# Modulation blocks 40 to 87 summed with multiply-adds on DVE during layer 0's feed-forward part, instead of matmuls on TensorE

## The chip, the cores and the metric

The kernel runs on one core of one Trainium2 chip. The metric is the device time of one execution in microseconds (us); lower is better. The engines are called PE (TensorE, with PEld for its weight loads), DVE (VectorE), ACT (ScalarE), POOL (GpSimd) and SP (SyncE, which here issues nearly all large loads).

## What is computed

Two layers of a transformer over 256 latent and 256 context tokens, width 1024, all in fp32. This case is about the modulation: for each layer, six vectors of 1024 numbers for each of two kinds of tokens.

```
silu_l = jax.nn.silu(c)
silu_c = jax.nn.silu(c_ctx)[None, :]
for layer in range(DEPTH):
    mod_l = split(silu_l @ mod_w[layer] + mod_b[layer], 6)
    mod_c = split(silu_c @ mod_w[layer] + mod_b[layer], 6)
    hl = modulate(rms_norm(xl, norm1_g[layer]), mod_l[0], mod_l[1])
    ...
    xl = xl + mod_l[2] * mix_l
    xl = xl + mod_l[5] * channel_mix(modulate(rms_norm(xl, norm2_g[layer]), mod_l[3], mod_l[4]))
    if need_ctx:          # layer 0 only; the same for xc with mod_c[2..5]
```

`channel_mix` is a SwiGLU of width 2816 in layer 0 (below: the feed-forward part) and a mixture of eight experts, two for each token, in layer 1. After layer 1's mixer the context tokens are no longer used.

## The kernel before

**Modulation.** Layers (`l`), vectors (`g`, 0 to 5) and slices of 128 inputs (`k`, 0 to 7) make 96 blocks of 128x1024 weights, 512 KB each, numbered j = 48 l + 8 g + k. `mod_load` issues a block's load on SP into a ring of buffers, named `rm` in the trace; `mod_ring` sets which buffers the ring has and up to which block it may load. A ring's buffer is loaded anew only when the block in it has been used. `tick()` uses one block: four matmuls on PE (line 458), in which `sc`, the two silu vectors padded to 32 columns, is the stationary operand and 256 columns of the block each are moved past it, added up over the eight k in one PSUM bank. After k = 7 `tick_end` copies the bank to SBUF on ACT (line 466), transposes it on PE (line 469) and adds the bias on DVE (line 473) into `modc`; `gain` (line 423) forms 1 + scale times the norm's gain.

**Where ticks stand.** Blocks 0 to 39 are used during layer 0's mixer. `norm_last`, the normalisation that ends a mixer or the feed-forward part, takes a pair of tick counts, one for each half of the tokens: (1, 3) ahead of the feed-forward part, and the rest up to block 71 after it. In the feed-forward part there is one tick after each of its blocks. Blocks 72 to 87 are used in layer 1's mixer, with a ring of one buffer, and 88 to 95 (layer 1, g = 5) behind it. A scheduler orders the code between `manual_schedule` sections and may bring ready instructions forward; each engine then runs its instructions in that order.

**The feed-forward part.** Weight blocks of 1 MB (`raw`) are loaded by SP into two buffers and split into a high part on ACT (`whi`, line 260) and a low part on DVE (`wlo`, line 273). Each product is three fp32r matmuls of 512 columns (`mm3`, lines 577 to 579). `FFN_PARTS` cuts the width 2816 in three parts; each has 4, 4 or 3 up-blocks b (256 columns of w1 and of w3: 96 matmuls each) and then four down-blocks. The first up-block is special: its input comes out of the normalisation just before, one k of eight at a time. For each k, `norm_pair` does two multiplications on DVE (`xn`, line 564), the high part on ACT (`hhi`, line 565), the low part on DVE (`hlo`, line 566), and then PE does the twelve matmuls of that k.

**Layer 1.** After the mixer the experts' weights, most of the kernel's bytes, are streamed in by SP. The first buffers for them come free when layer 1's scores (line 1407) have read `xT` for the last time, and when the mixer's pools close.

Of the kernel before, what the change touches and what calls it, by code (L numbers as in the profile page):

```python
# [10 lines left out]
F32 = mybir.dt.float32  # L11
# [4 lines left out]
OP = mybir.AluOpType  # L16
# [122 lines left out]
def program(tc, a, out):  # L139
    nc = tc.nc  # L140
    V, A, P, TE = nc.vector, nc.scalar, nc.gpsimd, nc.tensor
    uid = [0]

    def nm(s):
        uid[0] += 1
        return f"{s}_{uid[0]}"
# [12 lines left out]
    def bank(tag="m"):  # L159
        return ps.tile([128, 512], F32, name=nm("pm"), tag=tag, bufs=3 if tag == "m" else 1)  # L160
# [237 lines left out]
    def col(n, j, w=1):  # L398
        o = _OFF[n] + j
        return par[:, o:o + w]  # L400
# [17 lines left out]

    def gain(l, n):
        g = col('norm1_g' if n == 0 else 'norm2_g', 8 * l, 8)  # L420
        for s in range(2):
            c = 8 + 24 * n
            V.scalar_tensor_tensor(gm[:, l, n, s, :], modc[:, l, s, c:c + 8], 1.0, g, op0=OP.add, op1=OP.mult)

# [4 lines left out]
    def mod_ring(ring, upto):  # L429
        rings[:] = ring  # L430
        mst[3] = upto
        mod_load(mst[0] + len(ring) - 1)

    def mod_load(j):
        while mst[0] <= min(j, mst[3] - 1):
# [9 lines left out]
            mraw[mst[0]] = r  # L445
            mst[0] += 1

    def tick(n=1, end=True):

        for _ in range(n):  # L450
            j = mst[1]
            mst[1] += 1
            l, g, k = mods[j]
            if k == 0:
                mst[2] = bank("t")
            r = mraw.pop(j)
            for i in range(4):
                TE.matmul(mst[2][32 * i:32 * i + 32, :256], sc[:, k, :], r[:, i * 256:(i + 1) * 256],  # L458
                          start=k == 0, stop=k == 7)
            mod_load(j + len(rings))  # L460
            if k == 7 and end:
                tick_end()
# [588 lines left out]
    mx.close()  # L1051
    fx = ExitStack()
    ap = fx.enter_context(tc.tile_pool(name="ap", bufs=8, reuse_waits="tile"))
    mod_ring([(mq, "rm", 2)] * 2 + [(ap, "rm", 6)] * 6, 72)

    def resid1(l, n, d, p, s):
        u = HALVES[s]
# [35 lines left out]
    for m0, mn in FFN_PARTS:  # L1093
        act = []
        for b in range(mn // 2):
            if m0 + b == 0:
                p1, p3 = [bank(), bank()], bank2()
                h.append(norm_pair(pb, 0, 1, 0))
                for k in range(KD):
                    if k + 1 < KD:  # L1100
                        h.append(norm_pair(pb, 0, 1, k + 1))
                    for (bh, bl), pq in zip(first, (p1, (p3[:, 0, :], p3[:, 1, :]))):
                        for m in range(2):
                            c = slice(m * 128, m * 128 + 128)
                            mm3(pq[m], bh[:, k, c], bl[:, k, c], h[k][0], h[k][1], k == 0, k == KD - 1)
                ws.split_to(ws.pos[2])
                order.close()
            else:
                bh, bl = take()
                p1 = [bank(), bank()]  # L1110
                for m in range(2):
                    c = slice(m * 128, m * 128 + 128)
                    for k in range(KD):
                        mm3(p1[m], bh[:, k, c], bl[:, k, c], h[k][0], h[k][1], k == 0, k == KD - 1)
                bh, bl = take()
                p3 = bank2()
            for m in range(2):
                c = slice(m * 128, m * 128 + 128)
                s = ap.tile([128, T], F32, name=nm("fs"), tag="fs", bufs=2)
                A.activation(s, p1[m], AF.Silu)  # L1120
                if m0 + b:
                    for k in range(KD):
                        mm3(p3[:, m, :], bh[:, k, c], bl[:, k, c], h[k][0], h[k][1], k == 0, k == KD - 1)
                V.tensor_tensor(s, s, p3[:, m, :], op=OP.mult)
                n = len(act) % 4
                if n == 0:
                    ah, al = wide("ah"), wide("al")
                hi, lo = ah[:, n, :], al[:, n, :]
                hilo(hi, lo, s)
                act.append((hi, lo))  # L1130
            tick()
        for b in range(4):
            bh, bl = take()
            for m in range(2):
                c = slice(m * 128, m * 128 + 128)
                d = 2 * b + m
                p = bank()
                for k in range(mn):
                    mm3(p, bh[:, k, c], bl[:, k, c], act[k][0], act[k][1], k == 0, k == mn - 1)
                if m0 < 16:  # L1140
                    resid(0, 1, d, p)
                elif d < KD - 1:
                    if d == 0:
                        pn = norm_begin()
                    resid(0, 1, d, p)
                    norm_sq(pn, d)
            if m0 < 16 or b < 3:
                tick()
            if m0 == 16 and b == 0:
                warm_sqrt()  # L1150
    order = ExitStack()
    order.enter_context(tc.manual_schedule(engines=ENGINES))
    pb = norm_last(0, 1, p, pn, (1, 71 - mst[1]))
    fx.close()
    hx.close()

# [752 lines left out]
```

## Time and profile before

| | |
|---|---|
| median of 3 runs | 1715.19 us (1713.47 to 1717.45) |
| profiled execution, its own time | 1716.25 us |
| its span in the profile | 1714.2 us |
| PE busy | 1618.4 us, 94% of the span |
| DVE busy | 767.3 us, 45% |
| ACT busy | 580.5 us, 34% |
| chain that ended last | PE 67%, DMA 20%, DVE 8% |

A chain that ended last is followed back from the last instruction, at each step to what released it. A matmul in fp32 stands in the trace as two instructions, one in fp32r as one. Times in the rows below are counted from the span's start.

### The profile page before, as it was taken

How to read it: one execution, taken by the hardware profiler on the slowest of the kernel's cores; microseconds unless marked ns; L12 is line 12 of the kernel's file. 1: busy time of each engine (PE TensorE's matmuls, PEld its weight loads, DVE VectorE, ACT ScalarE, POOL GpSimd, SP SyncE). 2: the span in 40 equal slices, each digit the busy share in tenths (PEclk: the TensorE clock that was granted, in tenths of full speed). 3: DMA queues.
4: the chain of work that ended last, by engine and by line, in shares of the span. 5: the costliest groups of instructions: out<-in, count | busy, mean ns of one | idle time of the engine just before them, and what ended most of it. 6: DMA issues, size and time to landing. Idle time of an engine off the chain costs nothing.

```text
span 1714.2 us, 21413 instructions
## 1 busy us (share of the span) xinstructions
PE 1618.4 (94%) x8369; PEld 1029.0 (60%) x8369; DVE 767.3 (45%) x1214; ACT 580.5 (34%) x872; POOL 112.7 (7%) x81
## 2 busy tenths in 40 slices
PE   6898889999999999989999998999999899999986
PEld 2675667887777776776843434776343357843322
DVE  6679856333333235767730002885201068830001
ACT  3465743322222123554420103675000156630000
POOL 1433210000000000341000000000000000000000
PEclk9998999999999999999999999999999999999999
DMA  9535324223233333553599999998999999989997
GB/s 356 202 121 172 124 99 178 105 98 123 98 101 133 111 105 127 174 209 132 220 394 415 421 424 424 424 424 333 424 424 424 424 424 424 397 342 423 425 423 303
DMA packets 79278, 476.03 MB, mean 278 GB/s; under 512 B 8561, under 2 KB 12017, under 8 KB 31105
## 3 DMA queue, kind: packets, MB, share of 16 engines
q1 hardware_dynamic: 76544, 468.25, 68.8%
q0 software_dynamic: 1536, 5.28, 0.8%
q8 instruction: 68, 1.11, 0.3%
q10 hardware_dynamic: 1088, 1.05, 0.2%
q14 instruction: 42, 0.34, 0.1%
HBM read 471.40 MB, written 3.15 MB: 277 GB/s over the span
## 4 chain that ended last, share of the span: by engine, by line
PE 67%; DMA 20%; DVE 8%; issue 2%; ACT 2%; SPq 0%; POOL 0%; DVEq 0%; ACTq 0%
DMA raw<-in_moe_w_dram 18%; PE pm L1736 9%; PE pm L577 7%; PE pm L578 7%; PE pm L579 6%; PE p L578 5%; PE p L577 5%; PE p L579 5%; PE p L1736 4%; PE pm L1756 3%; PE pm L1758 3%; PE pm L1755 3%; PE pm L458 2%; PE pm L950 1%; PE pm L940 1%
## 5 line engine op out<-in xcount | busy, mean ns | idle before, releaser
L260 ACT ACTIVATE whi<-raw 128x1024 fp32r<-128x1024 f32 (+2 forms) x285 | 289.3, 1045 | 293.8 <-PE pm L578 115.3
L273 DVE TENSOR_TENSOR wlo<-raw,whi 128x1024 fp32r<-128x1024 f32 (+2 forms) x254 | 298.4, 1209 | 200.8 <-ACT whi L260 192.9
L1736 PE MATMUL pm<-raw,xs 128*64 128x512 f32 (+1 forms) x1432 | 308.6, 555 | 15.2 <-DMA raw<-in_moe_w_dram 14.7
L1736 PEld LDWEIGHTS pm<-raw,xs 128*64 128x64 f32 x1432 | 107.9, 138 | 196.7 <-issue 155.2
L1855 DVE TENSOR_TENSOR es<-es,pm 128x512 f32<-128x512 f32 (+1 forms) x38 | 24.5, 644 | 334.2 <-PE pm L1736 302.2
L1736 PE MATMUL p<-raw,ats 128*64 128x512 f32 x648 | 159.1, 598 | 4.3 <-DMA raw<-in_moe_w_dram 3.7
L273 POOL TENSOR_TENSOR wlo<-raw,whi 128x1024 fp32r<-128x1024 f32 (+1 forms) x31 | 75.4, 2444 | 560.0 <-ACT k L1236 486.0
L1767 ACT ACTIVATE ats<-pm 128x512 f32<-128x512 f32 (+1 forms) x24 | 13.1, 544 | 278.5 <-PE p L1736 242.0
L577 PE MATMUL pm<-hhi,whi 128*128 128x512 f32 x240 | 96.4, 407 | 3.8 <-ACT hhi L565 3.8
L1736 PEld LDWEIGHTS p<-raw,ats 128*64 128x64 f32 x648 | 46.1, 136 | 88.7 <-issue 72.0
L578 PE MATMUL pm<-hlo,whi 128*128 128x512 f32 x240 | 97.2, 405 | 1.0 <-DVE hlo L566 1.0
L579 PE MATMUL pm<-hhi,wlo 128*128 128x512 f32 x240 | 96.2, 402 | 0.0
L1756 PE MATMUL pm<-wlo,xe 128*128 128x512 f32 x224 | 92.4, 412 | 4.0 <-DVE wlo L273 4.0
L1755 PE MATMUL pm<-whi,xe 128*128 128x512 f32 x224 | 88.0, 399 | 3.1 <-ACT whi L260 3.1
L577 PE MATMUL p<-hhi,whi 128*128 128x512 f32 x224 | 89.0, 398 | 1.3 <-ACT hhi L556 0.7
L578 PE MATMUL p<-hlo,whi 128*128 128x512 f32 x224 | 89.1, 398 | 0.0
L579 PE MATMUL p<-hhi,wlo 128*128 128x512 f32 x224 | 88.8, 396 | 0.0
L1848 ACT ACTIVATE es<-pm 128x512 f32<-128x512 f32 (+1 forms) x38 | 21.3, 559 | 151.6 <-PE pm L1736 146.1
L458 PE MATMUL pm<-rm,sc 128*32 128x256 f32 x768 | 61.5, 408 | 10.2 <-DMA rm<-in_mod_w_dram 9.0
L577 PE MATMUL pm<-ah,whi 128*128 128x512 f32 x176 | 70.2, 402 | 0.0
L578 PE MATMUL pm<-al,whi 128*128 128x512 f32 x176 | 69.6, 397 | 0.0
L579 PE MATMUL pm<-ah,wlo 128*128 128x512 f32 x176 | 69.0, 396 | 0.0
(450 smaller groups left out, 2589.1 us busy)
## 6 DMA issues: line engine op xcount, KB each, us to landing
raw<-in_moe_w_dram SPq DMA_DIRECT2D x322, 1024.0 KB, 19.0
rm<-in_mod_w_dram SPq DMA_DIRECT2D x96, 512.0 KB, 4.6
raw<-in_ffn_w_dram SPq DMA_DIRECT2D x30, 1024.0 KB, 4.8
raw<-in_ab_w_in_dram SPq DMA_DIRECT2D x7, 1024.0 KB, 6.8
raw<-in_cd_w_in_dram SPq DMA_DIRECT2D x6, 1024.0 KB, 6.7
whi<-in_moe_w_dram SPq DMA_DIRECT2D x12, 512.0 KB, 15.3
raw<-in_ab_w_out_dram SPq DMA_DIRECT2D x4, 1024.0 KB, 5.2
raw<-in_cd_w_out_dram SPq DMA_DIRECT2D x4, 1024.0 KB, 4.9
```

The source lines that it names most:

```text
L260: x = A.activation(h, c, AF.Copy)
L273: x = low.tensor_tensor(l, r, h.bitcast(F32), op=OP.subtract)
L458: TE.matmul(mst[2][32 * i:32 * i + 32, :256], sc[:, k, :], r[:, i * 256:(i + 1) * 256], start=k == 0, stop=k == 7)
L577: TE.matmul(p, wh, xh, start=first, stop=False)
L578: TE.matmul(p, wh, xl, start=False, stop=False)
L579: TE.matmul(p, wl, xh, start=False, stop=last)
L1736: TE.matmul(o if len(w.shape) == 2 else o.rearrange("p (a b) -> p a b", b=S), x, w, start=start, stop=stop)
L1755: TE.matmul(p, xh[:, k, :], bh[:, k, :], start=hf == 0 and k == 0, stop=False)
L1756: TE.matmul(p, xh[:, k, :], bl[:, k, :], start=False, stop=False)
L1758: TE.matmul(p, xl[:, k, :], bh[:, k, :], start=False, stop=hf == 1 and k == 3)
L1848: A.activation(s[:, :w], p1[:, :w], AF.Silu)
L1855: V.tensor_tensor(s[:, :w], s[:, :w], p3[:, :w], op=OP.mult)
```

## The change

Blocks 40 to 87 go through a new function, `tick_dve`. For each block and each kind of token it multiplies the 128x1024 block by the kind's silu value of each partition and adds it to an accumulator `ma` of the same shape, on DVE. After k = 7, eight matmuls with a column of ones (each takes 128 columns of `ma` as stationary operand and moves one column) sum over the partitions and leave the vector in a PSUM bank, in the layout that `modc` has; no transpose follows. For layer 1 and g of 2 and above only the latent kind is computed. So 48 blocks become 9 first multiplications (`TENSOR_SCALAR`) and 63 multiply-adds (`SCALAR_TENSOR_TENSOR`) of 128x1024, and 9 sets of 8 ones-matmuls. All 48 blocks are placed in the feed-forward part (two ticks after an up-block, three after a down-block, four in the `norm_last` before it), with a ring of five buffers instead of eight. None are left in the `norm_last` after it and none of 72 to 87 in layer 1's mixer, since `tick` now returns when the ring's last block is used up.

```diff
     def gain(l, n):
         g = col('norm1_g' if n == 0 else 'norm2_g', 8 * l, 8)
-        for s in range(2):
+        for s in range(2 if l == 0 or n == 0 else 1):
...
+    ON_DVE, macc = range(40, 88), []
+
+    def tick_dve(j, l, g, k):
+
+        kinds = range(2 if l == 0 or g < 2 else 1)
+        if k == 0:
+            macc[:] = [ap.tile([128, 1024], F32, name=nm("ma"), tag=f"ma{s}", bufs=2 - s) for s in kinds]
+        r = mraw.pop(j)
+        for s in kinds:
+            if k == 0:
+                V.tensor_scalar(macc[s], r, sc[:, k, s:s + 1], None, op0=OP.mult)
+            else:
+                V.scalar_tensor_tensor(macc[s], r, sc[:, k, s:s + 1], macc[s], op0=OP.mult, op1=OP.add)
+        mod_load(j + len(rings))
+        if k < 7:
+            return
+        q = bank("t")
+        for s in kinds:
+            for i in range(8):
+                TE.matmul(q[:, 8 * s + i:8 * s + i + 1], macc[s][:, i * 128:(i + 1) * 128], ones[:, 0:1], start=True, stop=True)
+            V.tensor_tensor(modc[:, l, s, 8 * g:8 * g + 8], q[:, 8 * s:8 * s + 8], col('mod_b', 48 * l + 8 * g, 8), op=OP.add)
+        if g in (1, 4):
+            gain(l, g // 4)
+
     def tick(n=1, end=True):
 
         for _ in range(n):
             j = mst[1]
+            if j >= mst[3]:
+                return
             mst[1] += 1
             l, g, k = mods[j]
+            if j in ON_DVE:
+                tick_dve(j, l, g, k)
+                continue
...
-    mod_ring([(mq, "rm", 2)] * 2 + [(ap, "rm", 6)] * 6, 72)
+    mod_ring([(mq, "rm", 2)] * 2 + [(ap, "rm", 3)] * 3, 88)
...
-            tick()
+            tick(2)
...
-            if m0 < 16 or b < 3:
-                tick()
+            tick(3)
...
-    pb = norm_last(0, 1, p, pn, (1, 71 - mst[1]))
+    pb = norm_last(0, 1, p, pn, (0, 0))
```

Three places show how instructions move. The first is DVE at the normalisation ahead of the feed-forward part, before the change: the two reciprocals are followed at once by the first k's two `xn` and two `hlo`.

```order
L1058 SCALAR_TENSOR_TENSOR xT<-p_426_2416,modc,xT 128x256 x2
L551 RECIPROCAL rs_2446<-rs_2446 128x256 x2
L564 SCALAR_TENSOR_TENSOR xn_2488<-xT,gm,rs_2446 128x256
L564 SCALAR_TENSOR_TENSOR xn_2491<-xT,gm,rs_2446 128x256
L566 SCALAR_TENSOR_TENSOR hlo_2487<-xn_2488,modc,hhi_2486 128x256
L566 SCALAR_TENSOR_TENSOR hlo_2487<-xn_2491,modc,hhi_2486 128x256
```

And DVE at the same place in the changed kernel (all line numbers behind the new function are 29 higher; `ma_2449` and `ma_2450` are the accumulators of the two kinds for layer 0, g = 5):

```order
L580 RECIPROCAL rs_2440<-rs_2440 128x256
L460 SCALAR_TENSOR_TENSOR ma_2449<-rm_2143,sc,ma_2449 128x1024
L460 SCALAR_TENSOR_TENSOR ma_2450<-rm_2143,sc,ma_2450 128x1024
L460 SCALAR_TENSOR_TENSOR ma_2449<-rm_2145,sc,ma_2449 128x1024
L460 SCALAR_TENSOR_TENSOR ma_2450<-rm_2145,sc,ma_2450 128x1024
L460 SCALAR_TENSOR_TENSOR ma_2449<-rm_2147,sc,ma_2449 128x1024
L460 SCALAR_TENSOR_TENSOR ma_2450<-rm_2147,sc,ma_2450 128x1024
L593 SCALAR_TENSOR_TENSOR xn_2475<-xT,gm,rs_2440 128x256
L593 SCALAR_TENSOR_TENSOR xn_2478<-xT,gm,rs_2440 128x256
L460 SCALAR_TENSOR_TENSOR ma_2449<-rm_2149,sc,ma_2449 128x1024
L460 SCALAR_TENSOR_TENSOR ma_2450<-rm_2149,sc,ma_2450 128x1024
L595 SCALAR_TENSOR_TENSOR hlo_2474<-xn_2475,modc,hhi_2473 128x256
```

Two multiplications of block 40 (line 458) stand between the two reciprocals, and six multiply-adds now stand between the second reciprocal and the first `xn`, two more ahead of the first `hlo`. Behind these rows, ahead of the `hlo` of k = 1, 2 and 3 there are three, three and three more operations on `ma` (one of the nine a first multiplication), ahead of those of k = 4, 5, 6 and 7 one each (the third a first multiplication).

The second place is PE at the same normalisation, before: eight ticks stand between the sums for the norm and the first up-block's matmuls.

```order
L549 MATMUL p_427_2443<-sq_2447,ones 128x256
L458 MATMUL pm_2455<-rm_2143,sc 32x256 x4
L458 MATMUL pm_2455<-rm_2145,sc 32x256 x4
L458 MATMUL pm_2455<-rm_2147,sc 32x256 x4
L458 MATMUL pm_2455<-rm_2149,sc 32x256 x4
L458 MATMUL pm_2455<-rm_2151,sc 32x256 x4
L458 MATMUL pm_2455<-rm_2153,sc 32x256 x4
L458 MATMUL pm_2455<-rm_2155,sc 32x256 x4
L469 MATMUL pm_2455<-ident,stg 128x128 x2
L577 MATMUL pm_2483<-hhi_2486,whi_2368 128x512
```

And in the changed kernel:

```order
L571 MATMUL p_424_2437<-sa_2151,ones 128x256 x2
L578 MATMUL p_424_2437<-sq_2441,ones 128x256 x2
L606 MATMUL pm_2470<-hhi_2473,whi_2362 128x512
L607 MATMUL pm_2470<-hlo_2474,whi_2362 128x512
L608 MATMUL pm_2470<-hhi_2473,wlo_2364 128x512
```

Nothing stands there any more but the up-block itself.

The third place is PE later in the first up-block, where the changed kernel has the first vector's second set of ones-matmuls; here between the first and second matmul of k = 4.

```order
L606 MATMUL pm_2470<-hhi_2549,whi_2363 128x512
L467 MATMUL pm_2817<-ones,ma_2450 128x1 x8
L607 MATMUL pm_2470<-hlo_2550,whi_2363 128x512
L608 MATMUL pm_2470<-hhi_2549,wlo_2365 128x512
L606 MATMUL pm_2471<-hhi_2549,whi_2363 128x512
```

Before the change a tick stands in such places, every 48 or 96 matmuls of the feed-forward part:

```order
L579 MATMUL p_609_3726<-hhi_2628,wlo_3659 128x512
L458 MATMUL pm_3167<-rm_2961,sc 32x256 x4
L577 MATMUL pm_3803<-hhi_2486,whi_3716 128x512
L578 MATMUL pm_3803<-hlo_2487,whi_3716 128x512
L579 MATMUL pm_3803<-hhi_2486,wlo_3718 128x512
```

So the 18 ticks that stand in the feed-forward part's own stream (three of them and a piece of the fourth in the first up-block) become nine sets of eight ones-matmuls: two in the first up-block (the first set between the first and second matmul of k = 3), seven behind it.

## Rows read from the trace of the kernel before

**Rows 1.** Windows: us, busy us by engine, PE's clock, DMA share, GB/s.

```profile
291.00:678.00 387.00, 386.97 (x1736) 301.02 (x1734) 142.77 (x200) 105.61 (x137) 0.00 (x0) 1.00 0.34 119
678.00:836.00 158.00, 143.44 (x1018) 112.61 (x1018) 120.15 (x259) 79.43 (x169) 38.38 (x26) 0.96 0.43 149
836.00:1714.00 878.00, 835.33 (x4071) 437.73 (x4067) 294.37 (x372) 247.85 (x319) 5.66 (x5) 0.99 0.98 406
```

**Rows 2.** Chain of layer 1's mixer (684 to 836): lines, and three steps.

```profile
by line: DMA rm<-in_mod_w_dram 10.5%; PE p L1407 9.2%; PE pm L577 8.3%; PE pm L579 7.9%; PE pm L578 7.9%; PE pm L940 4.9%; PE pm L950 4.0%; DMA raw<-in_cd_w_in_dram 3.7%; PE p L577 3.1%; PE p L578 2.9%; PE pm L458 2.8%; PE p L579 2.8%; DVE 
...
728.36 4.82 DMA rm<-in_mod_w_dram
...
734.00 6.86 DMA rm<-in_mod_w_dram
...
782.98 4.24 DMA rm<-in_mod_w_dram
```

**Rows 3.** Timeline of SP's loads, end of layer 1's mixer.

```profile
827.93 0.62 SPq L208 DMA_DIRECT2D xT<-in_moe_w_dram  x1
...
835.92 3.63 SPq L214 DMA_DIRECT2D raw<-in_moe_w_dram  x6
```

**Rows 4.** Timeline of PE, first up-block: start us, us, what.

```profile
285.57 0.64 PE L458 MATMUL pm<-rm,sc 128*32 128x256 f32 x8
...
286.84 3.23 PE L458 MATMUL pm<-rm,sc 128*32 128x256 f32 x56
...
291.12 0.49 PE L577 MATMUL pm<-hhi,whi 128*128 128x512 f32 x1
...
314.02 0.39 PE L577 MATMUL pm<-hhi,whi 128*128 128x512 f32 x1
...
316.79 0.39 PE L577 MATMUL pm<-hhi,whi 128*128 128x512 f32 x1
```

**Rows 5.** Timeline of DVE, same stretch.

```profile
286.19 3.36 DVE L551 RECIPROCAL rs<-rs 128x256 f32<-128x256 f32 x2 [1.41 <-ACT rs L550]
289.47 0.78 DVE L564 SCALAR_TENSOR_TENSOR xn<-xT,gm,rs 128x256 f32<-128x256 f32 x2
...
296.73 0.88 DVE L566 SCALAR_TENSOR_TENSOR hlo<-xn,modc,hhi 128x256 fp32r<-128x256 f32 x2 [0.24 <-ACT hhi L565]
...
304.16 0.89 DVE L566 SCALAR_TENSOR_TENSOR hlo<-xn,modc,hhi 128x256 fp32r<-128x256 f32 x2 [0.18 <-ACT hhi L565]
```

**Rows 6.** List of lines: busy us, mean ns of one; idle before.

```profile
L857 DVE SCALAR_TENSOR_TENSOR lw<-a,lw 128x1024 f32<-128x1024 f32 x4 | 4.8, 1218 | 4.1 <-ACT a L856 4.1
```

**Rows 7.** Timeline of DVE elsewhere.

```profile
108.70 1.40 DVE L751 SCALAR_TENSOR_TENSOR u<-xr,par,u 128x512 f32<-128x512 f32 x2
...
776.87 0.88 DVE L931 TENSOR_SCALAR w<-w,sm 128x512 f32<-128x512 f32 x2
```

**Rows 8.** DMA issues, feed-forward part: count, KB each, median us to landing.

```profile
rm<-in_mod_w_dram SPq DMA_DIRECT2D x26, 512.0 KB, 4.2
```

**Rows 9.** Windows of 1 us, end of the feed-forward part.

```profile
686.00:687.00 1.00, 0.05 (x5) 0.06 (x5) 1.00 (x4) 0.14 (x1) 0.00 (x0) 0.58 0.26 102
...
691.00:692.00 1.00, 1.00 (x6) 0.98 (x6) 0.88 (x3) 0.48 (x2) 0.00 (x0) 0.50 0.02 8
...
693.00:694.00 1.00, 1.00 (x9) 0.72 (x12) 0.86 (x2) 1.00 (x2) 0.00 (x0) 1.00 0.00 0
```

**Rows 10.** Windows of line 458 alone, behind the first up-block and in layer 1.

```profile
317.00:678.00 361.00, 9.98 (x118) 2.59 (x118) 1.00 0.32 111
...
684.00:790.00 106.00, 10.67 (x128) 2.62 (x128) 0.94 0.58 202
```

**Rows 11.** Timeline of PE ahead of the experts.

```profile
861.72 0.61 PE L1527 MATMUL p<-ones,sq 128*128 128x1 f32 x4 [0.74 <-ACT sq L1522]
862.25 1.07 PE L458 MATMUL pm<-rm,sc 128*32 128x256 f32 x16
```

**Rows 12.** PE's waits in layer 1's mixer: us, times, longest.

```profile
PE pm L458 <- DMA rm<-in_mod_w_dram: 5.9, 5, 2.8
```

## The prediction

> **What bounds the kernel now.** Three stretches follow each other, and I read the windows first, because they show where PE has any air [rows 1]. In the feed-forward part (291 to 678 us) PE is busy for 386.97 of 387 us at full clock, while DVE works 143 us and the DMA engines a third of the time: whatever PE issues there beyond its own work lengthens the stretch one for one. Layer 1's mixer (678 to 836) is mixed: PE 143.4 of 158 us, with gaps. From 836 us on the DMA engines are busy 98% of the time at 406 GB/s, so the experts' stream bounds. The chain of the mixer shows what its gaps are [rows 2]: 10.5% of 152 us are loads of modulation blocks, three of them making 15.9 us, and 2.8% (4.3 us) ticks. The last view is SP's timeline at the mixer's end [rows 3]: the experts' loads start when `xT` and the mixer's buffers come free (827.9 and 835.9 us). A stream that is bound by its own bytes moves as a whole, so a mixer that ends later by d ends the kernel later by d.
>
> So three sums decide: the first up-block, the rest of the feed-forward part, and layer 1's mixer.
>
> **Term 1: the normalisation and the first up-block.** Before, eight ticks ran on PE at 285.6 to 290.1 us [rows 4], while DVE made its two reciprocals and the first `xn`, 286.2 to 290.3 [rows 5]. They cost nothing, so taking them away gives nothing there. What comes instead stands on DVE, which is what PE then waits for: ahead of the low part of k = 3, 19 operations of 128x1024, of which 16 multiply-adds and three first multiplications. A multiply-add of this shape took 1.22 us elsewhere [rows 6]; for 512 columns it takes 0.70 [rows 7], so the slope gives a fixed 0.18 us. With the same fixed part a first multiplication (0.44 us for 512 columns, same rows) takes 0.70; its bounds are 0.44 and 1.22. The 19 take 16 x 1.22 + 3 x 0.70 = 21.6 us. DVE waited some 0.2 us for ACT ahead of each of four `hlo` [rows 5]; it now works in these gaps, so I take off 0.8. The low part of k = 3, ready at 297.6 before, comes at 297.6 + 20.8 = 318.4.
>
> The blocks that DVE needs are no further delay: a load lands 4.2 us after its issue [rows 8], and a buffer that DVE frees is used again 5 to 12 us of DVE work later.
>
> PE's end of this up-block follows. One k took 2.77 us (314.02 to 316.79, twelve matmuls) [rows 4]. Eleven matmuls of k = 3 stand behind the late operand (2.5 us, to 320.9); k = 4 with eight ones-matmuls in it takes 2.8 + 2.1 (the 2.1 is priced in term 2), to 325.8; k = 5 to 7 end at 334.1. DVE keeps ahead there: with one operation more per k its last low part comes at 304.2 + 0.9 + 20.8 + three multiply-adds and a multiplication (4.4) = 330.3, and PE starts k = 7 at 331.3. Against 316.8 this is **+17.3 us**. The first set of ones-matmuls, inside k = 3, lies in PE's wait and costs nothing.
>
> The clock is a second part. PE now waits from about 287 us to the first high part, near 299, and then again and again. At the end of the feed-forward part the rows show the same thing small: after a stretch with PE busy 5% the clock is 0.58, five microseconds later still 0.50 with PE fully busy, and 1.00 two later [rows 9]; that is 1.2 and 2.4 GHz. At 1.2 GHz the first three k take 5.5 us each, which is about DVE's own pace there (three operations, `xn` and `hlo`: 5 us), so they stay hidden. It costs only if k = 3 still runs slow: 0 to 2.5 us. I take **+1.3**.
>
> **Term 2: the rest of the feed-forward part.** Removed: line 458 is busy 9.98 us there [rows 10], in 118 instructions or 14.75 ticks, and two pairs of transposes of about 0.15 us: -10.2, one for one, since PE never waits. Added: seven sets of eight ones-matmuls. The nearest row is two fp32 matmuls of one moving column ahead of the experts: the next matmul starts 0.53 us after they do [rows 11], 0.26 us each. So a set takes 2.1 us and seven take 14.8; if only half of it, 0.13, is what each costs in a row of eight, 7.4. Net **+4.6**, from -2.8 to +4.6 by these ends, and up to +7 if they cost a tenth more than the row (0.31).
>
> The page "TensorE: Matmul & The Clock Gate" of the Trainium skill (section "LDWEIGHTS (loading the stationary operand)") says that a weight load takes the number of its columns divided by 1.2, in ns, however little moves past it afterwards. An fp32 matmul loads 128 columns twice here, so an estimate by that page is 0.21 us each and 11.9 us for seven sets, against 14.8 from the row; the net would be +1.7. The rule speaks against this change in the same direction as the row: eight loads for eight columns.
>
> The multiply-adds behind the first up-block are hidden by PE: DVE had 143 us of 387 [rows 1], and 63 x 1.22 + 9 x 0.70 = 83 us in all leave it at 56% of the longer stretch. If that cover fails, the low parts of the weights (`wlo`) come late. Nearest to it is the second up-block: its first `wlo` now stands behind two multiply-adds, ready at 330.3 + 2.4 + 1.2 = 333.9, and PE wants it at 334.6. SP's queue has the third up-block's load behind eleven modulation loads, the last of which waits for a buffer until about 333; the block is wanted near 357, and PE would notice a delay of over 15 us.
>
> **Term 3: layer 1's mixer.** Sixteen ticks are gone, 10.67 us of PE [rows 10], and five waits of PE for their single buffer, 5.9 us in all, the longest 2.8 [rows 12]. The ticks in `norm_last` before it lay beside DVE's reciprocals, as in term 1, and give nothing. How much of the 16.6 us shortens the stretch? From below: each wait gives way to the next one just behind it (ACT's and DVE's work of the mixer); a quarter, 4 us, is left. From above: the whole share that the chain gives them, 15.9 + 4.3 = 20.2 [rows 2]. I take the middle, **-12 us**: all of the waits and a good half of the ticks, because PE was busy 91% of this stretch.
>
> **Sum.** 17.3 + 1.3 + 4.6 - 12 = +11.2 us. The profiled execution took 1716.25 us, so 1727.5 in its terms; it lay 1.06 us above the median of the three runs, so **1726.4 us** against 1715.19, 0.65% slower. A change of 0.2%, 3.4 us, is about what a measurement of this kernel can tell from none.
>
> **Rivals.**
>
> *Layer 1 pays for everything (not slower).* The chain names the block loads as what bounded the mixer at three places; if nothing stands close behind them, the mixer gains 20.2 us, and the sum is 1726.4 - 8.2 = 1718.2. For it: the chain passes through them. Against: in the time that a link of 6.86 us covers, PE was working on other matmuls, and its own waits there are 5.9 us, not 15.9. From a gain of 19.8 us on, the change is no longer slower than before. Chance 0.10.
>
> *The ones-matmuls cost half.* At 0.13 us each, 7.4 us less in term 2 and 1.0 in term 1: 1718.0. For it: in a row of eight, a weight load can run ahead of the matmul before it, as PEld does beside PE all through the feed-forward part. Against: there 512 columns move behind each load, here one. Chance 0.12.
>
> *The clock stays low through the first up-block.* If the waits keep PE at 1.2 GHz through all eight k, PE is the slow one from the first low part on (302 us): 302 + 8 x 5.5 + 2.1 = 348, 14 us beyond 334.1, and 1739 in all. For it: five microseconds of busy PE at 0.50 [rows 9]. Against: it went back to 1.00 right behind them. Chance 0.06. The same page (section "HAM oscillation — how this bites in real kernels") says that waits between bursts put PE back to its slow clock, so that each burst starts cold; by that rule this rival is the forecast.
>
> *DVE comes late again.* Further on up to eight multiply-adds stand in a row on DVE, 10 us, and a `wlo` behind them. If PE waits for it two or three times for 3 us, 1726.4 + 8 = 1734. For it: no more than 0.7 us of air at the second up-block. Against: DVE's 56%. Chance 0.12.
>
> *Both gains at once* (layer 1 in full and cheap ones-matmuls) would give 1710, faster. Chance 0.06.
>
> **How the numbers follow.** The forecast itself, with its terms as they stand, has 0.54 and its own range is 1721 to 1733. The first two rivals stand at 1718, at the edge of no change: half of their 0.22 falls within 0.2% of before. With a little of the main case's lower tail: faster 0.08, no change 0.14, slower 0.78. The range from 1715 to 1736 leaves out the clock's rival, the double gain, and part of the late DVE, together under 0.2.
>
> **What would show it.** Right: the second up-block's first matmul some 17 us later than before; ahead of it PE waiting for `hlo` and `hhi` while DVE is busy without a gap on `ma`; multiply-adds of about 1.22 us; sets of ones-matmuls of about 2.1 us each, with PE still busy all the time behind the first up-block; no loads of `rm` in layer 1's mixer, and its end, read against its start, 12 us shorter; the experts' first loads some 11 us later than 835.9, and the stream behind them as long as before. Wrong: a first up-block that ends less than 10 us later (the scheduler's order is not DVE's real order), waits of PE for `wlo` behind it, a granted clock under 1 there, or a mixer shorter by less than 4 or more than 20 us.

## The result and the profile after

The changed kernel takes 1731.94 us (median of 3 runs, 1730.58 to 1732.92), against 1715.19 before: ratio 1.0091, 95% interval 1.0077 to 1.0104, so 16.8 us slower. The profiled execution took 1731.94 us, with a span of 1729.8.

The same three stretches as in [rows 1], in windows of the changed kernel:

```profile
291.00:678.00 387.00, 373.32 (x1648) 302.34 (x1649) 213.58 (x260) 98.99 (x126) 0.00 (x0) 0.97 0.40 140
678.00:836.00 158.00, 135.22 (x788) 112.32 (x788) 120.86 (x244) 78.69 (x161) 39.09 (x27) 0.94 0.31 106
836.00:1714.00 878.00, 842.68 (x4169) 447.88 (x4169) 302.88 (x391) 254.04 (x332) 5.09 (x4) 0.99 0.98 405
```

PE is no longer busy throughout the first of them (373.3 of 387 us), DVE works 71 us more, and the clock is 0.97. Fixed stretches no longer hold the same work, though. To see where the time goes, each stage is measured from its own first event: the sums ahead of the feed-forward part, the end of the first up-block, the sums behind the feed-forward part, the first six of the experts' loads, the end. All are start times in the timelines of PE and SP.

| us | before | after | difference |
|---|---|---|---|
| start of the sums for the norm | 283.70 | 285.05 | +1.35, ahead of the change |
| norm and first up-block | 33.1 | 50.4 | +17.3 |
| rest of the feed-forward part | 361.0 | 361.4 | +0.4 |
| layer 1's mixer, to the experts' loads | 158.1 | 157.7 | -0.4 |
| from there to the end | 878.3 | 875.3 | -3.0 |
| span | 1714.2 | 1729.8 | +15.6 |

(The end of the first up-block is the start of the 97th matmul behind the sums. In the changed kernel two of these, 0.5 us, already belong to the second up-block, so its last own matmuls end at 335.87 and not at 335.42.) The first line and the last are not the change's: in the eleven profiled executions shown here the start lies between 283.5 and 286.2, and the last stage between 874.0 and 878.3 us, in no order that follows the kernels. What is left is one loss, and no gain in the mixer to set against it.

**The first up-block.** PE's timeline, which answers to [rows 4]; the brackets give how long PE sat idle and what ended it:

```profile
300.66 0.79 PE L606 MATMUL pm<-hhi,whi 128*128 128x512 f32 x1 [12.40 <-ACT hhi L594]
303.30 0.80 PE L607 MATMUL pm<-hlo,whi 128*128 128x512 f32 x1 [1.85 <-DVE hlo L595]
...
313.11 0.50 PE L607 MATMUL pm<-hlo,whi 128*128 128x512 f32 x1 [1.61 <-DVE hlo L595]
...
316.00 1.84 PE L467 MATMUL pm<-ones,ma 128*128 128x1 f32 x16
318.28 0.50 PE L607 MATMUL pm<-hlo,whi 128*128 128x512 f32 x1 [0.44 <-DVE hlo L595]
...
322.50 0.39 PE L606 MATMUL pm<-hhi,whi 128*128 128x512 f32 x1
...
335.87 0.39 PE L606 MATMUL p<-hhi,whi 128*128 128x512 f32 x1
```

And DVE's, which answers to [rows 5]:

```profile
287.54 1.75 DVE L580 RECIPROCAL rs<-rs 128x256 f32<-128x256 f32 x1 [1.41 <-ACT rs L579]
289.21 1.32 DVE L458 TENSOR_SCALAR ma<-rm,sc 128x1024 f32<-128x1024 f32 x2
290.44 1.75 DVE L580 RECIPROCAL rs<-rs 128x256 f32<-128x256 f32 x1
292.11 7.17 DVE L460 SCALAR_TENSOR_TENSOR ma<-rm,sc,ma 128x1024 f32<-128x1024 f32 x6
...
317.35 0.88 DVE L595 SCALAR_TENSOR_TENSOR hlo<-xn,modc,hhi 128x256 fp32r<-128x256 f32 x2
```

DVE has no gap from 289 to 330 us. The two reciprocals are apart by a pair of first multiplications, six multiply-adds follow (7.17 us, 1.20 each), and the low part of k = 3 is ready at 318.2 us, 33.2 us after the norm's sums began, where before it was 13.9. PE waits 12.4 us for the first high part and then for `hlo` three times; the next up-block's remaining matmuls start at 335.87. PE's clock over the same time, in windows (columns as in [rows 1]):

```profile
288.00:300.00 12.00, 0.26 (x2) 0.00 (x0) 12.00 (x13) 0.77 (x2) 0.00 (x0) 0.64 0.41 131
304.00:306.00 2.00, 2.00 (x6) 1.57 (x5) 2.00 (x4) 0.59 (x2) 0.00 (x0) 0.50 0.51 205
309.00:311.00 2.00, 2.00 (x10) 1.63 (x9) 2.00 (x3) 0.23 (x1) 0.00 (x0) 1.00 0.46 180
319.00:321.00 2.00, 2.00 (x6) 1.60 (x5) 2.00 (x6) 0.56 (x2) 0.00 (x0) 0.50 0.53 195
```

After the idle stretch the fully busy PE runs at 0.50 (1.2 GHz), and again in k = 3: a matmul there begins every 0.43 us instead of every 0.23. Ahead of this second stretch stand both two waits (1.61 and 0.44 us) and the first set of ones-matmuls (1.84 us); which of them made the clock fall is not separated.

**DVE's operations**, from the list of lines by shape (busy us, mean ns of one):

```profile
L460 DVE SCALAR_TENSOR_TENSOR ma<-rm,sc,ma 128x1024 f32<-128x1024 f32 x63 | 79.1, 1279 | 5.5 <-DMA rm<-in_mod_w_dram 5.1
...
L458 DVE TENSOR_SCALAR ma<-rm,sc 128x1024 f32<-128x1024 f32 x9 | 6.5, 737 | 0.0
```

The durations are 1279 and 737 ns; in a row they start every 1.20 and 0.66 us.

**A set of ones-matmuls** in the changed kernel, on PE's timeline:

```profile
432.06 0.39 PE L606 MATMUL pm<-ah,whi 128*128 128x512 f32 x1
432.30 1.84 PE L467 MATMUL pm<-ones,ma 128*128 128x1 f32 x16
434.00 0.48 PE L607 MATMUL pm<-al,whi 128*128 128x512 f32 x1
434.31 0.40 PE L608 MATMUL pm<-ah,wlo 128*128 128x512 f32 x1
```

Sixteen instructions (eight fp32 matmuls) take from 432.30 to 434.00, 1.70 us, and the matmul behind them needs 0.08 us more than usual before the next one starts: 1.78 us in all. An estimate from the figure for a weight load on the page "TensorE: Matmul & The Clock Gate" of the Trainium skill (section "LDWEIGHTS (loading the stationary operand)") is 2 x 107 ns, or 0.21 us for each matmul. The trace agrees: 1.70 us for eight is 0.21 each. The 0.26 us read from [rows 11], where two matmuls stood alone behind an idle PE, was too much. The other six sets behind the first up-block, some of them in two or three pieces, cost 1.77 to 1.78 us too. And a tick of the kernel before, the same way:

```profile
668.35 0.40 PE L579 MATMUL pm<-ah,wlo 128*128 128x512 f32 x1
668.68 0.64 PE L458 MATMUL pm<-rm,sc 128*32 128x256 f32 x8
669.25 0.50 PE L577 MATMUL pm<-ah,whi 128*128 128x512 f32 x1
669.59 0.40 PE L578 MATMUL pm<-al,whi 128*128 128x512 f32 x1
```

From 668.35 on, three matmuls would have taken 0.70 us; with the tick the fourth start is at 669.82 (0.23 after 669.59), so a lone tick costs 0.77 us, not the 0.68 of its busy time in [rows 10].

**Layer 1's mixer.** PE's waits in it (us in total, times, longest; line numbers of the changed kernel are 28 higher here), before (from the norm's sums to the experts' loads):

```profile
PE pm L458 <- DMA rm<-in_mod_w_dram: 5.9, 5, 2.8
PE pm L1265 <- DVE kn L1308: 1.8, 1, 1.8
...
PE pm L1257 <- DVE zt L1241: 1.0, 1, 1.0
```

and after:

```profile
PE pm L1285 <- DVE zt L1269: 4.2, 1, 4.2
PE p L606 <- ACT hcb L594: 3.8, 1, 3.8
PE pm L969 <- DVE sq L1378: 3.6, 2, 3.2
PE pm L1293 <- DVE kn L1336: 3.0, 1, 3.0
```

The waits for blocks are gone, and waits for DVE and ACT that were 1 to 2 us long or absent are 3 to 4 us long. In windows of the same stretch, before

```profile
677.78:835.92 158.14, 143.58 (x1017) 112.72 (x1017) 120.09 (x259) 79.35 (x169) 38.38 (x26) 0.96 0.43 149
```

and after

```profile
696.81:854.53 157.72, 134.94 (x862) 112.68 (x861) 124.40 (x256) 79.39 (x169) 39.09 (x27) 0.94 0.29 96
```

PE works 8.6 us less and idles 22.8 instead of 14.6 us. The ticks alone were busy 13.7 us in this stretch before (22 of them, six in the normalisation), so PE's other work got some 5 us longer: its clock is 0.94 instead of 0.96, and 21 more matmuls stand ahead of the stretch's end, behind `xT`. SP's loads, as in [rows 3]:

```profile
843.50 0.62 SPq L208 DMA_DIRECT2D xT<-in_moe_w_dram  x1
...
854.53 3.11 SPq L214 DMA_DIRECT2D raw<-in_moe_w_dram  x6
```

The experts' loads start 18.6 us later than 835.92. `xT` came free 15.6 us later, so against the 19.0 us by which the mixer began late, 3.5 were won up to there, and 3 of them given back behind it (11.0 us from the load of `xT` to the next six, against 8.0).

### The profile page after: what moved, and what is told of

It reads as the page before. It is cut to its first block, busy times and chain, and to the rows that moved or that the text cites. A ratio compares the mean times of both kernels' runs of the same rounds, so it can differ in the third digit from the quotient of the medians.

```text
span 1729.8 us, 20993 instructions
## 1 busy us (share of the span) xinstructions
PE 1608.3 (93%) x8117; PEld 1040.2 (60%) x8117; DVE 850.4 (49%) x1282; ACT 578.7 (33%) x866; POOL 112.8 (7%) x81
## 4 chain that ended last, share of the span: by engine, by line
PE 35%; DMA 17%; DVE 2%; issue 1%; ACT 0%; SPq 0%; DVEq 0%; ACTq 0%
DMA raw<-in_moe_w_dram 17%; PE pm L1764 9%; PE p L1764 4%; PE pm L1784 3%; PE pm L1786 3%; PE pm L1783 3%; PE p L607 2%; PE p L606 2%; PE p L608 2%; PE pm L606 1%; PE pm L607 1%; PE pm L608 1%; PE pm L1737 1%; PE p L1435 1%; PE pm L1792 1%; PE pm L1823 1%
## 5 line engine op out<-in xcount | busy, mean ns | idle before, releaser
L273 DVE TENSOR_TENSOR wlo<-raw,whi 128x1024 fp32r<-128x1024 f32 (+2 forms) x254 | 298.4, 1209 | 157.7 <-ACT whi L260 155.9
L460 DVE SCALAR_TENSOR_TENSOR ma<-rm,sc,ma 128x1024 f32<-128x1024 f32 x63 | 79.1, 1279 | 5.5 <-DMA rm<-in_mod_w_dram 5.1
```

Source lines behind the costliest of these rows:

```text
L273: x = low.tensor_tensor(l, r, h.bitcast(F32), op=OP.subtract)
L460: V.scalar_tensor_tensor(macc[s], r, sc[:, k, s:s + 1], macc[s], op0=OP.mult, op1=OP.add)
```

## Experiments

Ratios are those of the times against the kernel before, timed beside each. The stages are those of one profiled execution of each kernel, in us, as in the table above:

| | norm, first up-block | rest of feed-forward | mixer | ratio, 95% interval |
|---|---|---|---|---|
| before | 33.1 | 361.0 | 158.1 | |
| after | 50.4 | 361.4 | 157.7 | 1.0091 [1.0077, 1.0104] |
| e1_hold | 32.3 | 369.1 | 157.8 | 1.0050 [1.0034, 1.0066] |
| e2_mixer | 33.1 | 370.8 | 161.6 | 1.0049 [1.0032, 1.0066] |
| e3_part | 36.1 | 357.3 | 159.0 | 0.9996 [0.9985, 1.0007] |
| e4_ones2 | 49.7 | 385.2 | 158.2 | 1.0242 [1.0225, 1.0258] |
| e5_double | 394.1 (both) | | 171.4 | 1.0085 [1.0071, 1.0100] |
| e6_part8 | 30.0 | 356.1 | 159.1 | 0.9987 [0.9976, 0.9998] |
| e7_from48 | 30.0 | 361.4 | 155.1 | 0.9962 [0.9948, 0.9977] |
| e8_fillpe | 411.8 (both) | | 159.1 | 1.0115 [1.0098, 1.0132] |
| e9_filldve | 410.3 (both) | | 161.5 | 1.0134 [1.0117, 1.0151] |

**e1_hold: the same work on DVE, but behind the first up-block.**

```diff
-                V.tensor_scalar(macc[s], r, ...)
+                tc.keep_in_program_order(V.tensor_scalar(macc[s], r, ...))
...
-                V.scalar_tensor_tensor(macc[s], r, ...)
+                tc.keep_in_program_order(V.scalar_tensor_tensor(macc[s], r, ...))
...
-    pb = norm_last(0, 0, p, pn, (1, 3))
+    pb = norm_last(0, 0, p, pn, (0, 0))
```

> All 48 blocks are still summed on DVE in the feed-forward part, but none in the normalisation ahead of it, and each operation on ma is kept behind what stands ahead of it in the program, so that none gets ahead of an hlo of the first up-block. Theory A (the queue on DVE made the first up-block late): the stretch from the first reciprocal to the end of the first up-block, 30.6 us before and 47.9 to 49.2 us after the change, falls to 28 to 29 us, since the 3.25 ticks in it are gone too; behind it both of the first vector's sets of ones-matmuls now cost 1.7 to 1.8 us each, so about 18 us are won in all: 1714 us. Rival B (PE without ticks there runs at its low clock, and that makes the up-block late): the stretch stays above 40 us and the time above 1725 us. Rival C (DVE's bursts of multiply-adds delay wlo further on): PE's waits for wlo in the feed-forward part grow from none to 5 us or more, and the time is about 1720 us.

The norm and the first up-block shrank from 50.4 to 32.3 us (counted from the first reciprocal, 29.9 where 28 to 29 were expected): the queue on DVE had made it late. The slow clock alone is worth little there (the first k and a piece of the second still ran at 0.50, which used up what the 3.25 missing ticks gave). But the total is 1724.7 us, not 1714: the rest of the feed-forward part is 7.7 us longer than in the changed kernel. 3.6 us of it are the first vector's two sets; the others come from where the vector's end now stands (PE's timeline):

```profile
402.01 1.84 PE L467 MATMUL pm<-ones,ma 128*128 128x1 f32 x16
404.11 3.17 PE L467 MATMUL pm<-ones,ma 128*128 128x1 f32 x16 [0.26 <-DVE modc L468]
408.15 0.77 PE L606 MATMUL pm<-ah,whi 128*128 128x512 f32 x1 [0.87 <-DVE xT L1087]
```

The vector is wanted by the residual of the first down-block, and PE waits there for DVE, which waits for PE, and then runs at its low clock (0.77 us for a matmul of 512 columns). No wait for `wlo` appeared, so rival C falls.

**e2_mixer: the kernel before, without ticks in the mixer.**

```diff
-    mod_ring([(mq, "rm", 2)] * 2 + [(ap, "rm", 6)] * 6, 72)
+    mod_ring([(mq, "rm", 2)] * 2 + [(ap, "rm", 6)] * 6, 88)
...
-            tick()
+            tick(2)
...
-            if m0 < 16 or b < 3:
-                tick()
+            tick(2 if m0 == 0 else 1)
...
-    pb = norm_last(0, 1, p, pn, (1, 71 - mst[1]))
+    pb = norm_last(0, 1, p, pn, (1, 87 - mst[1]))
```

> The kernel before, with every block still on PE, but blocks 72 to 87 are used in the feed-forward part (16 ticks more there) and none in layer 1's mixer; the normalisation ahead of the mixer keeps its six ticks. Theory A (other waits stand close behind the loads, so that the mixer hardly gets shorter without its ticks): the feed-forward part gets longer by 16 ticks of 0.77 us and two vectors' ends, 12.9 us, the mixer shorter by about 3 us, as after the change; total 1725 us. Rival B (the mixer does get shorter by the forecast 12 us, and in the changed kernel the missing ticks in the normalisation ahead of it ate 9 us of that): mixer shorter by 12 us, total 1716 us.

1724.9 us: theory A's total, but partly by luck, since both of its terms missed, in opposite directions. In the profiled execution (1728.6 us, 3.7 above the median) the feed-forward part got longer by 9.8 us instead of 12.9, and the mixer did not get shorter at all (161.6 against 158.1 us; up to the load of `xT` it is 150.5 against 150.2). It shows three of the changed kernel's waits to the tenth of a microsecond, without any sums on DVE:

```profile
PE pm L1258 <- DVE zt L1242: 4.2, 1, 4.2
PE pm L942 <- DVE sq L1351: 3.6, 2, 3.2
PE pm L1266 <- DVE kn L1309: 3.0, 1, 3.0
```

So these waits come with the ticks' absence and not with the normalisation ahead; rival B falls. Why the mixer is 3.8 us longer up to `xT` than in the changed kernel (146.7), which has no ticks in the normalisation either, is not settled. The sixteen ticks cost 9.8 us in the feed-forward part, less than 16 x 0.77, since many stand in pairs, and a pair costs 1.20 us: its second tick pays no restart.

**e4_ones2: every ones-matmul twice.**

```diff
-            for i in range(8):
+            for i in list(range(8)) * 2:
                 TE.matmul(q[:, 8 * s + i:8 * s + i + 1], macc[s][:, i * 128:(i + 1) * 128], ones[:, 0:1], ...)
```

> The changed kernel with every ones-matmul done twice (same operands, same result). If one costs PE 0.21 us, the seven sets behind the first up-block add 7 x 1.70 = 11.9 us, the two in it another 1.3 to 3 us: 14 us over the changed kernel, 1746 us. If it costs 0.26 us, as the prediction took: 17.5 us, 1749.5 us. If it costs 0.13 us: 8.7 us, 1740.5 us.

25.5 us over the changed kernel, more than any of the prices. A double set takes 3.57 us on PE's timeline, twice 1.78, so the price of 0.21 us stands. The sum built on it does not. Only one of the first vector's two sets stayed in the first up-block, so eight double sets stand behind it where the changed kernel has seven single ones: 8 x 3.57 - 7 x 1.78 = 16.1 us of the 23.8 by which the rest of the feed-forward part got longer. The other 7.7 go with the clock, whose mean over the rest is 0.98 (first line) against 1.00 in the changed kernel (second line); 0.02 of 385 us is about as much:

```profile
333.96:719.16 385.20, 385.07 (x1746) 314.78 (x1744) 185.62 (x221) 92.60 (x114) 0.00 (x0) 0.98 0.38 134
335.42:696.81 361.39, 361.27 (x1602) 292.66 (x1600) 180.08 (x216) 93.06 (x115) 0.00 (x0) 1.00 0.40 141
```

Behind the double set that begins at 457.08 us the feed-forward matmuls run at 0.57, though PE is busy without a gap; behind the one that begins at 435.71 they run at 1.00:

```profile
461.00:465.00 4.00, 4.00 (x13) 3.10 (x12) 4.00 (x7) 0.00 (x0) 0.00 (x0) 0.57 1.02 416
439.30:443.30 4.00, 4.00 (x19) 3.22 (x19) 3.89 (x6) 0.30 (x1) 0.00 (x0) 1.00 0.48 142
```

Seven times 28 or 32 instructions of the sets stand in a row there. Behind four of these runs the next six to eleven matmuls are slow, behind three none is; behind the single sets of the changed kernel's rest none is either.

**e3_part and e6_part8: only blocks 48 to 63 on DVE.** In e3_part six buffers hold the loads and two accumulators stand beside them:

```diff
-    ON_DVE, macc = range(40, 88), []
+    ON_DVE, macc = range(48, 64), []
...
-    mod_ring([(mq, "rm", 2)] * 2 + [(ap, "rm", 3)] * 3, 88)
+    mod_ring([(mq, "rm", 2)] * 2 + [(ap, "rm", 4)] * 4, 72)
```

with the calls of `tick` as before the change, and the operations on `ma` held as in e1_hold.

> Only blocks 48 to 63 on DVE (four sets of ones-matmuls), with their operations kept in the program's order; 40 to 47 and 64 to 87 stay on PE where they were before. By the theory (a tick in the feed-forward part costs PE 0.77 us, a set of eight ones-matmuls 1.78 us, and DVE's own work is hidden as long as it stands behind the first up-block): 16 ticks and two ends go, 12.3 + 0.6 us, four sets come, 7.1 us, so 5.5 to 6 us faster than before, 1709.5 us. Rival (the operations on DVE hold up wlo, or the loads on SP are late with six buffers instead of eight): no gain, 1715 us or more, with PE waiting in the feed-forward part.

No gain, and the reason was the rival's second one. PE's timeline at the normalisation:

```profile
287.15 2.37 PE L487 MATMUL pm<-rm,sc 128*32 128x256 f32 x40
290.17 0.64 PE L487 MATMUL pm<-rm,sc 128*32 128x256 f32 x8 [0.65 <-DMA rm<-in_mod_w_dram]
294.11 1.08 PE L487 MATMUL pm<-rm,sc 128*32 128x256 f32 x8 [3.30 <-DMA rm<-in_mod_w_dram]
```

The seventh and eighth tick have no buffer to be loaded into ahead of time; PE waits 3.3 us for the last, and the up-block starts late and at the low clock (36.1 us instead of 33.1). The rest of the feed-forward part gained 3.7. In e6_part8 the eight buffers are kept for blocks 40 to 47, the accumulators take two of them later, and blocks 64 to 71 all stand in the normalisation behind:

```diff
-            macc[:] = [ap.tile(..., tag=f"ma{s}", bufs=1) for s in kinds]
+            macc[:] = [ap.tile(..., tag="rm", bufs=6) for s in kinds]
...
+            if j == 47:
+                mod_ring([(mq, "rm", 2)] * 2 + [(ap, "rm", 6)] * 4, 72)
...
+        if j == 63:
+            mod_ring([(mq, "rm", 2)] * 2 + [(ap, "rm", 6)] * 6, 72)
```

> As the kernel in which only blocks 48 to 63 were on DVE, but with eight buffers for blocks 40 to 47 as before (the accumulators take over two of them later), and all of blocks 64 to 71 in the normalisation behind the feed-forward part. By the prices measured so far, against before: first up-block 3.25 ticks less, -2.7 us; rest of the feed-forward part 14.75 ticks of 0.77 us and two ends less, four sets of 1.78 us more, -4.9 us; the normalisation with two ticks more, 0 to +1 us: together 6.5 to 7.5 us faster, ratio about 0.996. Rival (what a tick costs PE is hidden somewhere, or DVE's operations make wlo late): no faster than before.

The stages came out as priced: -3.1, -4.9 and +1.0 us. Over twelve runs, which spread from 1707 to 1717 us, the kernel is 0.13% faster than before (0.02 to 0.24%), less than the 0.4% that the stages of its profiled execution promise. That execution, 1707.11 us, was the fastest of the twelve, whose median is 1711.56; why its runs spread more than others stays open.

**e7_from48: the change without its first vector.**

```diff
-    ON_DVE, macc = range(48, 64), []
+    ON_DVE, macc = range(48, 88), []
...
-                mod_ring([(mq, "rm", 2)] * 2 + [(ap, "rm", 6)] * 4, 72)
+                mod_ring([(mq, "rm", 2)] * 2 + [(ap, "rm", 6)] * 4, 88)
```

(against e6_part8, without its second `mod_ring` after block 63; `tick(2)`, `tick(3)` and `norm_last(0, 1, p, pn, (0, 0))` as in the change)

> The change without its first vector: blocks 40 to 47 are ticks on PE with eight buffers, as before; 48 to 87 are summed on DVE in the feed-forward part, behind the first up-block, and none are left in layer 1's mixer or the normalisation ahead of it. By the prices measured so far, against before: first up-block -2.7 us, rest of the feed-forward part -11.4 - 0.6 + 7 x 1.78 = +0.5 us, mixer 0 to -0.5 us: about 2 us faster than before, so that the first vector alone accounts for the change's loss. Rival (the sums on DVE cost more than their sets of ones-matmuls, or the mixer needs the ticks' absence for something): slower than before by 4 us or more.

1708.5 us, 0.38% or 6.5 us faster than before where 2 were expected, and the fastest kernel of this study. The first up-block is 3.1 us shorter than before and the rest 0.4 longer, as priced. The mixer came out 3 us shorter where 0 to 0.5 was expected; it has the same operations as in the changed kernel (157.7 us), in a slightly other order. PE's waits for `zt`, `hcb`, `sq` and `kn` are the changed kernel's to 0.1 us. Of the 2.7 us between the two, 2.0 lie behind the load of `xT` (9.05 us against 11.03), where SP's next load starts behind an earlier group of line 979's matmuls; why the order came out so, no run separates. The loss of the change is its first vector.

This kernel also shows what the eight ticks in the normalisation did. The first up-block holds neither ticks nor ones-matmuls in e1_hold and here; with the eight ticks on PE ahead of it, it takes 30.0 us from the norm's sums on, without them 32.3. PE's clock in the first k, here and then in e1_hold:

```profile
291.00:295.00 4.00, 3.97 (x17) 3.01 (x18) 3.39 (x11) 1.82 (x4) 0.00 (x0) 1.00 1.02 390
293.00:297.00 4.00, 4.00 (x10) 3.14 (x10) 3.50 (x9) 1.82 (x4) 0.00 (x0) 0.50 0.00 0
```

**e5_double, e8_fillpe, e9_filldve: what sets the mixer.** e5_double is the kernel before with the sixteen ticks of the mixer doing their matmuls twice:

```diff
+            n2 = 2 if 72 <= j < 88 else 1
             for i in range(4):
-                TE.matmul(..., start=k == 0, stop=k == 7)
+                for t in range(n2):
+                    TE.matmul(..., start=k == 0 and t == 0, stop=k == 7 and t == n2 - 1)
```

> The kernel before, with each of the sixteen ticks of layer 1's mixer doing its four matmuls twice (the sum is halved when it is copied out, so the result stays): 64 fp32 matmuls more on PE, 9 to 10 us of PE work, no load more. Theory A (PE has air there, since the mixer is set by DVE's and ACT's work and the loads arrive in it): at most 3 us longer. Rival B (PE is what sets the mixer, and a tick costs its own 0.64 us): 9 us or more longer.

The mixer is 13.2 us longer: theory A as I had put it is wrong. Work that is added to PE in the mixer of the kernel before is paid in full. In windows and waits:

```profile
678.76:850.11 171.35, 156.42 (x1145) 118.44 (x1145) 122.17 (x259) 79.86 (x169) 38.89 (x26) 0.96 0.39 137
```

```profile
PE pm L460 <- DMA rm<-in_mod_w_dram: 9.0, 5, 2.8
```

PE is busy 12.8 us more, and its waits for the single buffer, which now comes free later, rise from 5.9 to 9.0 us, while others shrink; this run does not separate PE's work from the buffer's turn. Together with e2_mixer: more PE work is paid for, less is not paid back. That would fit two chains of nearly one length, PE's with its ticks and DVE's, which hand over to each other. The last two kernels test it in the changed kernel, where the ticks are gone, with work that nobody reads, put where the ticks stood:

```diff
+        p = bank("t")
+        for i in range(4):
+            tc.keep_in_program_order(TE.matmul(p[32 * i:32 * i + 32, :256], sc[:, 0, :], row[:, :256], start=True, stop=True))
```

> The changed kernel with work put into layer 1's mixer that nobody reads: where a tick stood, four fp32 matmuls of 256 columns on PE, sixteen times, over a constant row instead of a block, so that nothing is loaded (10 us of PE work). What is open after the runs so far: without its ticks the mixer hardly gets shorter, yet doubled ticks lengthen it by 13 us. Theory A (DVE's chain is almost as long as PE's; without the ticks PE waits for it and has air again): at most 4 us longer than the changed kernel, PE's waits for zt, kn and sq shrink. Rival B (PE sets the mixer in the changed kernel too, and something else of the change made it slower): 9 to 11 us longer.

```diff
+        w = nw.tile([128, 2], F32, name=nm("fl"), tag="fl", bufs=2)
+        tc.keep_in_program_order(V.tensor_reduce(w[:, 0:1], row[:, 0:512], axis=AX.X, op=OP.add))
```

> The same with DVE: where a tick stood, one sum over 512 columns of a constant row on DVE, sixteen times, about 10 us of DVE work. Theory A (DVE's chain now sets the mixer): 8 to 11 us longer than the changed kernel, nearly the whole of it. Rival B (PE sets it): at most 4 us longer.

e8_fillpe:

```profile
697.96:857.10 159.14, 142.15 (x974) 111.97 (x972) 121.89 (x254) 78.67 (x167) 39.20 (x27) 0.95 0.28 95
```

e9_filldve:

```profile
694.82:856.33 161.51, 135.58 (x846) 113.75 (x844) 132.86 (x270) 79.00 (x167) 39.41 (x27) 0.92 0.27 94
```

With 7.2 us more of busy PE the mixer is 1.4 us longer (3.4 up to the load of `xT`): PE has air that it did not have before the change. Of the three waits, those for `sq` and `kn` shrink from 3.6 and 3.0 us to 0.5 and 1.0, that for `zt` stays at 4.1. Up to `xT` this kernel takes 150.1 us and the kernel before 150.2, so sixteen pieces of PE work without a load make the stretch as long as sixteen ticks that wait 5.9 us for theirs (the six ticks in the normalisation differ, too). With 8.5 us more of busy DVE it is 3.8 us longer (5.8 up to `xT`). So DVE weighs more than PE there now, but about a third to a half of its work, too, found a gap. Theory A holds for PE; that DVE alone sets the mixer does not. Which other steps (ACT's halves of the splits, the waits back and forth) take the rest is not settled.

## Why the prediction was right, and where it was wrong

The forecast, slower by 11.2 us with a range of 1715 to 1736, held; the main step was right, and two others were off and partly cancelled each other. That the time fell into the range is in part luck: with the mixer's miss alone, 11.6 us, it would have been 1738 us.

**The first up-block (+17.3 and +1.3 forecast, +17.3 measured in all).** Right, and by its mechanism: the low part of k = 3 was forecast for 318.4 and came at 318.2, with a start that was 1.35 us later, so the queue cost 1.5 us less than forecast; e1_hold took the queue away, and the stretch fell by 18.0 us. The multiply-adds start every 1.20 us (1.22 taken). The clock's part was 1.7 us: 4.2 us from the late low part in k = 3 to the start of k = 4, against 2.5. One reason was wrong without harm here: that the eight ticks "cost nothing, so taking them away gives nothing there". Taking them away costs 2.3 us through the clock (e7_from48 against e1_hold); in the changed kernel this lay hidden behind DVE's queue.

**The rest of the feed-forward part (+4.6 forecast, +0.4 measured).** The mechanism was right, two sizes were off. A set costs 1.78 us, not 2.1: the Trainium skill's rule was nearer than the row I took (and the 0.31 us of the upper end is a fifth above that row, not a tenth). And a tick costs 0.77 us, not its busy 0.68, since the stream of matmuls around it also loses its step; the busy time of line 458 was the wrong measure of what its removal gives. The multiply-adds behind the first up-block were hidden, as forecast: no wait of PE for `wlo` shows there.

**Layer 1's mixer (-12 forecast, -0.4 measured).** This is the step that failed: "all of the waits and a good half of the ticks, because PE was busy 91% of this stretch". The trace showed that PE waited for loads; it could not show how closely other waits stood behind. They took the whole gain: PE's idle time rose by 8.2 us while its work fell by 8.6. A mixer shorter by less than 4 us was one of the prediction's own signs of being wrong. e2_mixer shows that this needs nothing of the change but the ticks' absence; e5_double that with a busy share of 91% every addition to PE (and to its wait for the buffer) was paid for; e8_fillpe that without the ticks it no longer is. A gain read from a chain or from a sum of waits has an upper bound there, and the lower end of 4 us was not low enough.

**The stream.** Right: the experts' loads started 17.3 us later, less the later start, and the end moved with them within the 4 us by which this stage varies.

Of the rivals, "layer 1 pays for everything" is out, and "the ones-matmuls cost half" too; the clock fell as its rival said, but for two pieces of the up-block only.

## What to carry to other kernels

Work for an idle engine is free only if its queue, at that place, feeds nobody: 21 us of multiplications and multiply-adds on a DVE that is idle almost two thirds of the time cost 17 us, since they stood ahead of the operands that PE was waiting for; for the other vectors, behind that point, the same work cost PE its ones-matmuls and nothing else, as long as their end did not stand just ahead of its reader, as in e1_hold. A wait that is taken away is worth what lies behind it: before counting on it, take the waiting work out in an experiment and look which waits grow. And price a short insertion in a stream of matmuls by the start times on either side of it, not by its busy time.

## What the runs showed of the hardware that was not expected

Matmuls of one moving column keep PE busy in the profile, but its clock could fall behind long runs of them. In e4_ones2, behind 32 instructions in a row (3.6 us) that began at 457.08, the granted clock was 0.57 over the next 4 us of gapless matmuls of 512 columns, so that most of them ran at 1.2 GHz; of seven such runs of 28 or 32 instructions, four were followed by slow matmuls and three were not. Behind the changed kernel's runs of at most 16 (1.8 us) in the rest of the feed-forward part it stayed at 1.00. This is some 7.7 of the 25.5 us that doubling the ones-matmuls cost.
